# Norms of the first 768 tokens ranked among the last columns' FFN tiles, and a short convolution that starts chunk by chunk

## The chip, the cores and the metric

The kernel runs on one core of a Trainium2 chip. The metric is the device time of one execution in microseconds (us). Before the change it is 2387.01 us, the median of three runs (2381.73, 2387.01 and 2387.42).

## The reference, cut to what matters

The program is one inference step of a two-layer decoder trunk on 1032 tokens: 1024 of a prompt and 8 samples. Each layer is a mixer and a SwiGLU FFN, both closed by a LayerNorm over 1024 channels:

```
x = layernorm(ALPHA * x + mixer(x),  ln_mix_w[l], ln_mix_b[l])
x = layernorm(ALPHA * x + (silu(x @ w1) * (x @ w3)) @ w2,  ln_ffn_w[l], ln_ffn_b[l])
# mixer of layer 1, the short convolution:
p = x @ w_in                       # 1024 -> 3 * 1024: bg, cg, xv
y = bg * conv3(cg * xv);  mixer = y @ w_out
```

All of it is float32. The change touches the LayerNorm that closes the FFN in both layers, and the first tiles of the short convolution.

## The kernel before

**Data.** Activations lie transposed, channels on the 128 partitions, in three chunks of tokens: chunk 0 is tokens 0 to 383, chunk 1 is 384 to 767, chunk 2 is the other 264. `r0`, `r1` and `r2` hold the residual stream of each chunk (8 slices of 128 channels). Each float32 operand is split into a high and a low part that TensorE takes in its fast float32 form (`split`, L119: a cast on ScalarE, ACT, for the high part, a subtraction on VectorE, DVE, for the low part; both have line L120 or L121). A product is three matmuls: high weight by low activation, low by high, high by high (L141 to L143). `x0ha, x0hb, x0la, x0lb` are the parts of chunk 0's normalised input, `x1..` those of chunk 1, `x2h, x2l` those of chunk 2.

**Weights.** `load_unit` (L123) fetches one unit of 128x1024 weights (512 KB, on SyncE's queue SP) and splits it into `wh` (ACT) and `wl` (DVE). There are four buffers `raw` for the fetched units and three each for `wh` and `wl`. The first matmul of each unit reads `wl`.

**The FFN's main part.** `main_g` does chunks 0 and 1 (with fewer products, by sums of parts). Then the loop of `main` (L753) does chunk 2 in groups of four tiles of 128 hidden columns, the last group with two: `up` (L291 on DVE multiplies by silu, L283 on ACT; then the parts `hb` are split) and `down` (L266 on DVE adds to `r2`). A tile of `up` is two weight units of 24 matmuls each; a `down` of four tiles is four units, two output slices each of 12 matmuls. Layer 0 has 10 such tiles, so three groups; layer 1 has 18, so five.

**The norm.** `normalise` (L196) is a chain over engines: DVE adds the slices (L202 to L205), TensorE sums over channels (L206), DVE subtracts the mean (L216, four instructions), ACT squares (L223), DVE adds the squares (L225, L228), TensorE sums them (L231), DVE scales (L193), GpSimd (POOL) takes the power -0.5 (L194), TensorE spreads the result over the partitions (L239), DVE multiplies (L242, four instructions). Then `layer_norm` applies weight and bias (L252 on DVE, L254 on ACT) and, in layer 0, splits the eight slices for the next product (L120, L121); in layer 1 it stores them (L258).

**What sets the order.** The program is built in the order of the code, each instruction with a running number, its rank (`tc.cur_priority`). A scheduler then lays each engine's instructions in one fixed order: by its own estimate of when operands are ready, the lowest rank first. On the chip every engine works off its list in that order. Before the change the norms of chunks 0 and 1 are written after the first and the second group of the loop (L757), and so ranked there; the norm of chunk 2 comes last (L759).

**The short convolution.** `mix1` (L816) makes one tile of 128 channels: three weight units, each applied to the chunks it is given. Tiles 0 and 1 (`M1` is 2) are done for chunks 0 and 1 together (L843), then for chunk 2 alone (L845); the other tiles for all three chunks at once.

Of the kernel before, what the change touches and what calls it, by code (L numbers as in the profile page):

```python
# [31 lines left out]
NF = DFF // P  # L32
# [14 lines left out]
M1 = 2  # L47
# [21 lines left out]
def trunk(ctx: ExitStack, tc: tile.TileContext, xT, win0, wout0, win1, wout1, w1, w3, w2, vecs, sh, scf, ssc,  # L69
# [21 lines left out]
    def xp(k, c):  # L91

        if c == 2:
            return x2h[:, k, :], x2l[:, k, :]
        return X[c][k // 4][:, k % 4, :], X[c][2 + k // 4][:, k % 4, :]
# [23 lines left out]
    def split(hi, lo, src):  # L119
        SC.copy(hi, src)  # L120
        VE.tensor_tensor(lo, src, hi.bitcast(F32), ALU.subtract)  # L121

    def load_unit(src, kt, n=NK):  # L123

        wh = wsp.tile([P, NK, P], F32R, name="wh")
        wl = wsp.tile([P, NK, P], F32R, name="wl")
        raw = wsp.tile([P, NK * P], F32, name="raw", bufs=R_BUFS).rearrange("p (k f) -> p k f", f=P)
        src = src.rearrange("p (k f) -> p k f", f=P)
        for k in range(0, kt, n):
            e = min(k + n, kt)  # L130
            nc.sync.dma_start(raw[:, k:e], src[:, k:e])
            split(wh[:, k:e], wl[:, k:e], raw[:, k:e])
        return wh, wl, kt

    def mm(unit, c, parts=None):

        wh, wl, kt = unit
        ps = mmp.tile([P, 512], F32, name="mm")[:, :CH[c][1] - CH[c][0]]
        for k in range(kt):
            h, l = (parts or xp)(k, c)  # L140
            PE.matmul(ps, wl[:, k, :], h, start=k == 0, stop=False)  # L141
            PE.matmul(ps, wh[:, k, :], l, start=False, stop=False)  # L142
            PE.matmul(ps, wh[:, k, :], h, start=False, stop=k == kt - 1)  # L143
        return ps
# [44 lines left out]
    def col(i):  # L189
        return vec[:, i:i + 1]  # L190
# [113 lines left out]
    with tc.tile_pool(name="hg", bufs=1) as hg, tc.tile_pool(name="hg2", bufs=2) as hg2:  # L304
# [244 lines left out]
        for token in SCRIPT.split():  # L549
            op, gs = token[0], {"b": (1, 2)}.get(token[-1]) or (int("0" + token[1:][-1:]),)  # L550
            g, i = gs[0], int("0" + token[1:-1])
# [27 lines left out]
    ALL = (0, 1, 2)  # L579
# [12 lines left out]
    class Swiglu:  # L592
# [157 lines left out]
        def main(self, first, out):  # L750

            self.main_g(first)
            for j, m in enumerate(range(first, NF, 4)):  # L753
                ms = list(range(m, min(m + 4, NF)))
                self.up(ms, (2,))
                self.down(ms, (2,))
                if j < 2:  # L757
                    self.norm(j, out)
            self.norm(2, out)  # L759

    def t_pair(pool, j):
# [3 lines left out]
    with tc.tile_pool(name="t0", bufs=1, reuse_waits="tile") as tp:  # L765
        F0.T2, F0.T3 = t_pair(tp, 2), t_pair(tp, 3)
        with tc.tile_pool(name="head0", bufs=1, reuse_waits="tile") as act:
# [6 lines left out]
            for m in range(0, NEARLY, 4):  # L774
# [4 lines left out]
                p = tc.cur_priority  # L779
                F0.down(ms, (1, 2))  # L780
        with tc.tile_pool(name="main0", bufs=1, reuse_waits="tile") as act:
            F0.T4 = t_pair(act, 4)
            F0.main_pool(act)
            q = tc.cur_priority
# [6 lines left out]
    with tc.tile_pool(name="act", bufs=H_BUFS, reuse_waits="tile") as act:  # L791
        stt = act.tile([P, NK, 2, NS], F32, name="stt", bufs=1)
        nc.sync.dma_start(stt, ssc)
        nws = act.tile([P, NK, 2, NS], F32, name="nws", bufs=1)
        SC.copy(nws[:, :, 0, :], stt[:, :, 1, :])
        nwp = act.tile([P, NK, 2], F32, name="nwp", bufs=1)
        zhist = act.tile([P, NK, 2], F32, name="zhist", bufs=1)
        ys = {}

        def taps(i, c, z, y):  # L800

            w0, w1_, w2_ = (col(V_SC + 8 * j + i) for j in range(3))
            w = CH[c][1] - CH[c][0]
            e = w - NS if c == 2 else w
            VE.tensor_scalar(y, z[:, 2:2 + w], w2_, None, ALU.mult)
            for d, wd in ((1, w1_), (2, w0)):
                lo = d if c == 0 else 0
                VE.scalar_tensor_tensor(y[:, lo:e], z[:, 2 + lo - d:2 + e - d], wd, y[:, lo:e], ALU.mult, ALU.add)
            if c == 2:
                s = y[:, e:w]  # L810
                VE.scalar_tensor_tensor(s, stt[:, i, 1, :], w1_, s, ALU.mult, ALU.add)
                VE.scalar_tensor_tensor(s, stt[:, i, 0, :], w0, s, ALU.mult, ALU.add)
                SC.copy(nws[:, i, 1, :], z[:, 2 + e:2 + w])
                SC.copy(nwp[:, i, :], z[:, e:2 + e])

        def mix1(i, chunks):  # L816
            zs = {}
            u = load_unit(win1[8 + i], NK)
            for c in chunks:
                w = CH[c][1] - CH[c][0]  # L820
                zs[c] = act.tile([P, 386], F32, name="sl", bufs=SL_BUFS)[:, :2 + w]
                SC.copy(zs[c][:, 2:], mm(u, c))
            u = load_unit(win1[16 + i], NK)
            for c in chunks:
                z = zs[c]
                VE.tensor_tensor(z[:, 2:], mm(u, c), z[:, 2:], ALU.mult)
                if c:
                    SC.copy(z[:, 0:2], zhist[:, i, :])
                if c < 2:
                    SC.copy(zhist[:, i, :], z[:, 384:386])  # L830
                y = act.tile([P, 384], F32, name=f"y{i}{c}", tag=("hh", "hl")[(3 * i + c) % 2])
                ys[i, c] = y[:, :CH[c][1] - CH[c][0]]
                taps(i, c, z, ys[i, c])
            u = load_unit(win1[i], NK)
            for c in chunks:
                y = ys[i, c]
                VE.tensor_tensor(y, mm(u, c), y, ALU.mult)

        def parts_of(c):
            for k in range(NK):  # L840
                split(*xp(k, c), ys[k, c])

        for i in range(M1):  # L843
            mix1(i, (0, 1))
        for i in range(M1):  # L845
            mix1(i, (2,))
        for i in range(M1, NK - 1):
            mix1(i, ALL)
        for c in ALL:
            mix1(NK - 1, (c,))  # L850
            parts_of(c)
        nc.sync.dma_start(ss_o, nws)
        nc.sync.dma_start(sp_o, nwp)

    F1 = Swiglu(1)
    with tc.tile_pool(name="t1", bufs=1, reuse_waits="tile") as tp:
        F1.T2, F1.T3 = t_pair(tp, 2), t_pair(tp, 3)
        with tc.tile_pool(name="head1", bufs=1, reuse_waits="tile") as act:
# [10 lines left out]
            p = tc.cur_priority  # L869
            F1.down(ms, ALL, ALL)  # L870
        with tc.tile_pool(name="main1", bufs=1, reuse_waits="tile") as act:
            F1.T4 = t_pair(act, 4)
            F1.main_pool(act)
            q = tc.cur_priority
# [74 lines left out]
```

## Time and profile before

| what | us |
|---|---|
| median of three runs | 2387.01 |
| the profiled execution | 2385.06 |
| its span, from the first to the last instruction | 2383.2 |
| TensorE (PE) busy | 2333.2 |
| DVE busy | 1701.4 |
| ACT busy | 874.2 |

In the span, layer 0's FFN does chunk 2 from 1166.5 to 1273.6 us, and the short convolution begins there. Layer 1's FFN does chunk 2 from 2198.7 to about 2364 us. The profile gives every instruction's start, its duration, and the idle time of its engine before it with what ended that wait. Starts on one engine are a little closer than durations say, since instructions overlap at their ends.

### The profile page before, as it was taken

Reading aid. Unit: us, or ns where it says so; the run is one execution under the profiler, and the core shown is the slowest. Engines: PE = TensorE matmul, PEld = TensorE weight load, DVE = VectorE, ACT = ScalarE, POOL = GpSimd, SP = SyncE. Lnnn points to the kernel's source line nnn. Section 1 sums busy time; section 2 is a strip of 40 time slices with the busy share of each in tenths; the row PEclk is TensorE's granted clock in tenths of the full one; section 3 lists DMA queues with packets and bytes.
Section 4 is the critical chain, followed back from the end, with each engine's and each line's share of the span. In section 5 each row is a group of like instructions: output and inputs, shape, how many; then the busy total and the mean of one; then the engine's idle time right before and its main releaser. Section 6 shows DMA issues by size and latency. Waiting matters only on the chain.

```text
span 2383.2 us, 36586 instructions
## 1 busy us (share of the span) xinstructions
PE 2333.2 (98%) x14974; PEld 2293.0 (96%) x14974; DVE 1701.4 (71%) x2943; ACT 874.2 (37%) x1479; POOL 45.3 (2%) x40
## 2 busy tenths in 40 slices
PE   9999999999899999999998999999999999999997
PEld 8999899999899999999998999999999999999997
DVE  8998789897863336777686423667957777777775
ACT  5434353335631223332354211435513332332553
POOL 0000000000000000000000000000000000000000
PEclk9999999999999999999999999999999999999998
DMA  5322222453341221222342311334402222132663
GB/s 186 116 78 73 88 78 77 123 167 113 116 131 45 79 73 48 68 80 71 119 149 88 90 53 45 90 115 142 133 27 71 63 80 68 57 89 80 194 196 98
DMA packets 85560, 229.79 MB, mean 96 GB/s; under 512 B 8225, under 2 KB 26401, under 8 KB 85137
## 3 DMA queue, kind: packets, MB, share of 16 engines
q1 hardware_dynamic: 85232, 227.02, 30.9%
q8 instruction: 117, 1.92, 0.3%
q0 software_dynamic: 160, 0.45, 0.1%
q14 instruction: 51, 0.41, 0.1%
HBM read 220.22 MB, written 7.21 MB: 95 GB/s over the span
## 4 chain that ended last, share of the span: by engine, by line
PE 91%; DVE 4%; ACT 2%; POOL 1%; DMA 1%; issue 1%; SPq 0%; POOLq 0%; DVEq 0%; ACTq 0%
PE mm L141 23%; PE mm L142 23%; PE mm L143 23%; PE mm L692 6%; PE mm L693 6%; PE mm L691 6%; PE sm L335 2%; DVE wl L121 1%; POOL rs L194 1%; PE sm L239 1%; DVE r L216 1%; DVE acc L225 1%; ACT r L254 0%; PE sm L382 0%; ACT wh L120 0%
## 5 line engine op out<-in xcount | busy, mean ns | idle before, releaser
L120 ACT CAST wh<-raw 128x1024 fp32r<-128x1024 f32 (+1 forms) x466 | 468.6, 1007 | 899.4 <-PE mm L143 607.5
L121 DVE TENSOR_TENSOR wl<-raw,wh 128x1024 fp32r<-128x1024 f32 (+1 forms) x466 | 544.1, 1169 | 230.4 <-ACT wh L120 226.5
L141 PE MATMUL mm<-x2h,wl 128*128 128x264 f32 x1216 | 349.7, 288 | 7.0 <-DVE wl L121 6.9
L143 PE MATMUL mm<-x2h,wh 128*128 128x264 f32 x1216 | 346.8, 285 | 0.0
L142 PE MATMUL mm<-x2l,wh 128*128 128x264 f32 x1216 | 346.3, 285 | 0.0
L266 DVE TENSOR_TENSOR r<-r,mm 128x384 f32<-128x384 f32 (+1 forms) x336 | 171.5, 521 | 99.6 <-PE mm L143 99.2
L141 PEld LDWEIGHTS mm<-x2h,wl 128*128 128x128 f32 x1216 | 229.8, 189 | 9.6 <-DVE wl L121 8.3
L142 PEld LDWEIGHTS mm<-x2l,wh 128*128 128x128 f32 x1216 | 230.0, 189 | 1.6 <-issue 0.8
L143 PEld LDWEIGHTS mm<-x2h,wh 128*128 128x128 f32 x1216 | 229.1, 188 | 0.1
L141 PE MATMUL mm<-hb,wl 128*128 128x384 f32 (+1 forms) x672 | 211.4, 320 | 8.4 <-ACT hb L120 4.8
L142 PE MATMUL mm<-hb,wh 128*128 128x384 f32 (+1 forms) x672 | 213.1, 319 | 0.0
L143 PE MATMUL mm<-hb,wh 128*128 128x384 f32 (+1 forms) x672 | 212.8, 318 | 0.0
L482 DVE SCALAR_TENSOR_TENSOR cc<-r,vec,cc 128x256 f32<-128x256 f32 (+17 forms) x360 | 189.7, 561 | 0.9
L141 PEld LDWEIGHTS mm<-hb,wl 128*128 128x128 f32 x672 | 125.9, 190 | 10.7 <-ACT hb L120 7.0
L141 PE MATMUL mm<-x0ha,wl 128*128 128x384 f32 x384 | 132.7, 346 | 1.9 <-DVE wl L121 1.9
L143 PE MATMUL mm<-x0ha,wh 128*128 128x384 f32 x384 | 133.2, 347 | 0.0
L142 PE MATMUL mm<-x0la,wh 128*128 128x384 f32 x384 | 132.3, 345 | 0.8 <-DVE x0la L121 0.8
L143 PE MATMUL mm<-x0hb,wh 128*128 128x384 f32 x384 | 132.0, 344 | 0.0
L141 PE MATMUL mm<-x0hb,wl 128*128 128x384 f32 x384 | 131.3, 342 | 0.0
L142 PE MATMUL mm<-x0lb,wh 128*128 128x384 f32 x384 | 131.0, 341 | 0.0
L143 PE MATMUL mm<-x1hb,wh 128*128 128x384 f32 x384 | 130.8, 341 | 0.0
L142 PE MATMUL mm<-x1lb,wh 128*128 128x384 f32 x384 | 130.5, 340 | 0.0
(310 smaller groups left out, 5242.8 us busy)
## 6 DMA issues: line engine op xcount, KB each, us to landing
raw<-in_w SPq DMA_DIRECT2D x256, 512.0 KB, 3.7
raw<-in_win SPq DMA_DIRECT2D x88, 512.0 KB, 3.7
raw<-in_wout SPq DMA_DIRECT2D x48, 512.0 KB, 3.6
raw<-in_w SPq DMA_DIRECT2D x16, 256.0 KB, 2.7
out_yT<-r SPq DMA_DIRECT2D x8, 384.0 KB, 3.4
S0t<-in_sh SPq DMA_DIRECT2D x8, 256.0 KB, 3.2
out_hs<-S0t SPq DMA_DIRECT2D x8, 256.0 KB, 2.0
r<-in_xT SPq DMA_DIRECT2D x4, 384.0 KB, 7.5
```

The source lines that it names most:

```text
L120: SC.copy(hi, src)
L121: VE.tensor_tensor(lo, src, hi.bitcast(F32), ALU.subtract)
L141: PE.matmul(ps, wl[:, k, :], h, start=k == 0, stop=False)
L142: PE.matmul(ps, wh[:, k, :], l, start=False, stop=False)
L143: PE.matmul(ps, wh[:, k, :], h, start=False, stop=k == kt - 1)
L194: GP.tensor_tensor(dst, dst, mhalf[:p, :n], ALU.pow)
L266: VE.tensor_tensor(v, v, ps, ALU.add)
L335: PE.matmul(ps[:sr, c * 64:(c + 1) * 64].rearrange("p (b i) -> p b i", i=hh), kp[:, c * P:c * P + sr], qr, start=True, stop=True)
L482: VE.scalar_tensor_tensor(acc[:, lo:W], u[:, 30 + lo - d:30 + W - d], col(V_DW + (30 - d) * 4 + i), acc[:, lo:W], ALU.mult, ALU.add)
L691: PE.matmul(ps, w[1][:, k], t[0][:, k], start=k == 0, stop=False)
L692: PE.matmul(ps, w[0][:, k], t[1][:, k], start=False, stop=False)
L693: PE.matmul(ps, w[0][:, k], t[0][:, k], start=False, stop=k == 3)
```

## The change

The loop over chunk 2's groups has no norm in it any more. After the loop the norms of chunks 0 and 1 are written with a rank of their own: one third and two thirds of the way from the loop's first rank to its last. In the short convolution, tiles 0 and 1 are done for chunk 0, then for chunk 1, then for chunk 2, each time with the weight units loaded anew: 18 units in place of 12.

```diff
             self.main_g(first)
-            for j, m in enumerate(range(first, NF, 4)):
+            p = tc.cur_priority
+            for m in range(first, NF, 4):
                 ms = list(range(m, min(m + 4, NF)))
                 self.up(ms, (2,))
                 self.down(ms, (2,))
-                if j < 2:
-                    self.norm(j, out)
+            q = tc.cur_priority
+            for c in (0, 1):
+                tc.cur_priority = p + (q - p) * (c + 1) // 3
+                self.norm(c, out)
+            tc.cur_priority = q
             self.norm(2, out)
...
-        for i in range(M1):
-            mix1(i, (0, 1))
-        for i in range(M1):
-            mix1(i, (2,))
+        for c in ALL:
+            for i in range(M1):
+                mix1(i, (c,))
```

The order on DVE shows what this does. In it `r0_73`, `r1_5697` and `r2_74` are the residuals of chunks 0, 1 and 2, `mm_` is a result of TensorE, `wl_` the low part of a weight unit, `hb_` a part of a hidden tile, `acc_` and `sq_` sums and squares of a norm.

**Place 1, layer 0, the `down` of the first group.** DVE before:

```order
L266 TENSOR_TENSOR r2_74<-r2_74,mm_11564 128x264
L266 TENSOR_TENSOR r2_74<-r2_74,mm_11578 128x264
L121 TENSOR_TENSOR wl_11725<-raw_11726,wh_11724 128x1024
L266 TENSOR_TENSOR r2_74<-r2_74,mm_11598 128x264
L266 TENSOR_TENSOR r2_74<-r2_74,mm_11612 128x264
L121 TENSOR_TENSOR wl_11758<-raw_11759,wh_11757 128x1024
L266 TENSOR_TENSOR r2_74<-r2_74,mm_11632 128x264
L266 TENSOR_TENSOR r2_74<-r2_74,mm_11646 128x264
L216 TENSOR_TENSOR r0_73<-r0_73,sm_11661 128x768 x4
```

And now:

```order
L266 TENSOR_TENSOR r2_74<-r2_74,mm_11564 128x264
L266 TENSOR_TENSOR r2_74<-r2_74,mm_11578 128x264
L216 TENSOR_TENSOR r0_73<-r0_73,sm_12287 128x768 x4
L225 TENSOR_TENSOR acc_12295<-acc_12295,sq_12299 128x768
L266 TENSOR_TENSOR r2_74<-r2_74,mm_11598 128x264
L266 TENSOR_TENSOR r2_74<-r2_74,mm_11612 128x264
L266 TENSOR_TENSOR r2_74<-r2_74,mm_11632 128x264
L225 TENSOR_TENSOR acc_12295<-acc_12295,sq_12303 128x768
L266 TENSOR_TENSOR r2_74<-r2_74,mm_11646 128x264
L121 TENSOR_TENSOR wl_11661<-raw_11662,wh_11660 128x1024
```

The norm of chunk 0 starts two weight units earlier, in the middle of the group; the split of the next `up`'s first unit, which stood ahead of the norm (`wl_11725`), now stands behind its L216, two L225 and four L266 (`wl_11661`).

**Place 2, layer 0, the end of chunk 1's norm.** DVE before, beside the last `up`:

```order
L193 TENSOR_SCALAR rs_12144<-sm_12143 96x4
L121 TENSOR_TENSOR wl_12378<-raw_12376,wh_12377 128x1024
L242 TENSOR_TENSOR r1_5697<-r1_5697,sm_12167 128x768 x4
L252 TENSOR_SCALAR r1_5697<-r1_5697,vec_133 128x384
L121 TENSOR_TENSOR x1la_81<-r1_5697,x1ha_79 128x384 x2
L291 TENSOR_TENSOR hb_12275<-mm_12308,hb_12275 128x264
L121 TENSOR_TENSOR x1la_81<-r1_5697,x1ha_79 128x384 x2
L121 TENSOR_TENSOR x1lb_82<-r1_5697,x1hb_80 128x384
L121 TENSOR_TENSOR wl_12488<-raw_12489,wh_12487 128x1024
L121 TENSOR_TENSOR x1lb_82<-r1_5697,x1hb_80 128x384 x2
L121 TENSOR_TENSOR hb_12335<-hb_12275,hb_12334 128x264
```

And now, beside the `down` of the second group:

```order
L193 TENSOR_SCALAR rs_12358<-sm_12357 96x4
L121 TENSOR_TENSOR wl_12073<-raw_12074,wh_12072 128x1024
L242 TENSOR_TENSOR r1_5697<-r1_5697,sm_12381 128x768 x4
L252 TENSOR_SCALAR r1_5697<-r1_5697,vec_133 128x384
L121 TENSOR_TENSOR x1la_81<-r1_5697,x1ha_79 128x384 x4
L121 TENSOR_TENSOR x1lb_82<-r1_5697,x1hb_80 128x384
L266 TENSOR_TENSOR r2_74<-r2_74,mm_12024 128x264
L266 TENSOR_TENSOR r2_74<-r2_74,mm_12044 128x264
L266 TENSOR_TENSOR r2_74<-r2_74,mm_12058 128x264
L121 TENSOR_TENSOR x1lb_82<-r1_5697,x1hb_80 128x384 x2
L121 TENSOR_TENSOR wl_12106<-raw_12107,wh_12105 128x1024
```

The norm of chunk 1 now ends before the last `up` (`wl_12073` is that `up`'s first unit, `wl_12106` its second); the last hidden tile's L291 and `hb` no longer stand among its instructions.

**Place 3, layer 1, the end of chunk 0's norm.** DVE before, beside an `up`:

```order
L193 TENSOR_SCALAR rs_21246<-sm_21245 96x4
L121 TENSOR_TENSOR wl_21462<-raw_21463,wh_21461 128x1024
L242 TENSOR_TENSOR r0_73<-r0_73,sm_21269 128x768 x4
L252 TENSOR_SCALAR r0_73<-r0_73,vec_133 128x384
L291 TENSOR_TENSOR hb_21365<-mm_21398,hb_21365 128x264
L121 TENSOR_TENSOR wl_21498<-raw_21499,wh_21497 128x1024
```

And now, beside the `down` of the second group:

```order
L193 TENSOR_SCALAR rs_22732<-sm_22731 96x4
L266 TENSOR_TENSOR r2_74<-r2_74,mm_21556 128x264
L266 TENSOR_TENSOR r2_74<-r2_74,mm_21570 128x264
L266 TENSOR_TENSOR r2_74<-r2_74,mm_21590 128x264
L242 TENSOR_TENSOR r0_73<-r0_73,sm_22755 128x768 x4
L252 TENSOR_SCALAR r0_73<-r0_73,vec_133 128x384
L266 TENSOR_TENSOR r2_74<-r2_74,mm_21604 128x264
L266 TENSOR_TENSOR r2_74<-r2_74,mm_21624 128x264
L266 TENSOR_TENSOR r2_74<-r2_74,mm_21638 128x264
L121 TENSOR_TENSOR wl_21654<-raw_21652,wh_21653 128x1024
```

The norm has moved from an `up` into a `down`, and the split of that `down`'s last unit (`wl_21654`) stands behind the norm's L242.

## Rows read from the trace of the kernel before

**Rows 1.** The page: busy time, share of the span and instructions of each engine.
```profile
PE 2333.2 (98%) x14974; PEld 2293.0 (96%) x14974; DVE 1701.4 (71%) x2943; ACT 874.2 (37%) x1479; POOL 45.3 (2%) x40
```

**Rows 2.** Waits, 1189 to 1274 us: who, for whom, total us, times, longest.
```profile
PE mm L141 <- DVE hb L291: 3.3, 1, 3.3
PE mm L141 <- ACT hb L120: 2.7, 1, 2.7
...
PE mm L141 <- DVE wl L121: 2.2, 2, 1.6
```

**Rows 3.** Waits of PE, 2183 to 2365 us, chunk 2 of layer 1.
```profile
PE sm L239 <- POOL rs L194: 2.1, 2, 1.0
```

**Rows 4.** Timeline of PE: start, us, instruction, count, [idle before <-releaser].
```profile
1224.40 0.39 PE L141 MATMUL mm<-x2h,wl 128*128 128x264 f32 x1 [1.64 <-DVE wl L121]
...
1228.15 0.39 PE L141 MATMUL mm<-x2h,wl 128*128 128x264 f32 x1 [0.58 <-DVE wl L121]
...
1263.30 0.59 PE L141 MATMUL mm<-hb,wl 128*128 128x264 f32 x1 [3.34 <-DVE hb L291]
...
1267.03 1.25 PE L141 MATMUL mm<-hb,wl 128*128 128x264 f32 x4 [2.70 <-ACT hb L120]
```

**Rows 5.** Timeline of DVE, the same places, columns as in rows 4.
```profile
1262.82 0.42 DVE L291 TENSOR_TENSOR hb<-mm,hb 128x264 f32<-128x264 f32 x1
...
1267.01 0.43 DVE L121 TENSOR_TENSOR hb<-hb 128x264 fp32r<-128x264 f32 x1 [0.19 <-ACT hb L120]
```

**Rows 6.** Windows: stretch, us, busy (count) of PE PEld DVE ACT POOL, PEclk, DMA, GB/s.
```profile
1189.69:1201.54 11.85, 11.82 (x99) 11.60 (x98) 8.23 (x13) 4.52 (x5) 0.00 (x0) 1.00 0.60 178
1262.60:1272.50 9.90, 6.50 (x28) 6.19 (x29) 7.77 (x17) 5.84 (x12) 0.00 (x0) 0.50 0.21 61
620.70:624.10 3.40, 3.40 (x18) 3.40 (x18) 3.00 (x4) 0.14 (x1) 0.00 (x0) 0.51 0.71 195
1216.20:1219.60 3.40, 3.40 (x31) 3.40 (x30) 3.12 (x4) 2.61 (x5) 0.00 (x0) 1.00 0.49 158
...
1202.00:1268.00 66.00, 55.64 (x439) 53.54 (x438) 59.18 (x86) 42.42 (x67) 3.91 (x2) 0.96 0.46 139
1300.00:1325.00 25.00, 25.00 (x146) 25.00 (x145) 9.04 (x13) 4.57 (x9) 0.00 (x0) 1.00 0.26 85
```

**Rows 7.** Timeline of DVE, 1195 to 1222 us: `down`, then the norm of chunk 0.
```profile
1195.72 0.76 DVE L266 TENSOR_TENSOR r<-r,mm 128x264 f32<-128x264 f32 x2
...
1202.38 3.54 DVE L216 TENSOR_TENSOR r<-r,sm 128x768 f32<-128x768 f32 x4 [0.22 <-PE sm L206]
1205.85 0.95 DVE L225 TENSOR_TENSOR acc<-acc,sq 128x768 f32<-128x768 f32 x1
...
1213.17 1.23 DVE L121 TENSOR_TENSOR wl<-raw,wh 128x1024 fp32r<-128x1024 f32 x1
1216.48 3.55 DVE L242 TENSOR_TENSOR r<-r,sm 128x768 f32<-128x768 f32 x4 [2.09 <-PE sm L239]
...
1220.33 1.02 DVE L121 TENSOR_TENSOR x0la<-r,x0ha 128x384 fp32r<-128x384 f32 x2
```

**Rows 8.** Timeline of POOL, the power -0.5 of chunk 0's norm.
```profile
1213.30 1.96 POOL L194 TENSOR_TENSOR rs<-rs,mhalf 96x4 f32<-96x4 f32 x1 [573.09 <-DVE rs L193]
```

**Rows 9.** Timeline of PE, the matmul L239 that waits for it, chunks 0, 1, 2.
```profile
1215.31 1.13 PE L239 MATMUL sm<-ident,rs 96*128 96x96 f32 x8 [1.04 <-POOL rs L194]
...
1256.86 0.91 PE L239 MATMUL sm<-ident,rs 96*128 96x96 f32 x6 [1.04 <-POOL rs L194]
...
1288.58 0.90 PE L239 MATMUL sm<-ident,rs 88*128 88x88 f32 x6 [0.22 <-POOL rs L194]
```

**Rows 10.** Timeline of ACT beside that norm: the cast of a weight unit.
```profile
1201.73 1.05 ACT L120 CAST wh<-raw 128x1024 fp32r<-128x1024 f32 x1 [1.82 <-PE mm L143]
```

**Rows 11.** Timeline of PE, two other waits.
```profile
548.80 0.88 PE L239 MATMUL sm<-ident,rs 96*128 96x96 f32 x3 [2.12 <-POOL rs L194]
...
619.77 0.39 PE L141 MATMUL mm<-x2h,wl 128*128 128x264 f32 x1 [3.62 <-DVE wl L121]
```

## The prediction, made before the changed kernel ran

> **What bounds the kernel now.** I read the engines' busy shares first: PE is busy 2333 of 2383 us, so what can be won lies in some 50 us of PE's idle time and in stretches at a lower clock [rows 1]. Next the waits of PE, window by window. In layer 0's last chunk (1189 to 1274 us) it waits four times over for DVE's or ACT's splits (8.2 us) and twice for POOL [rows 2, 9]; in layer 1's last chunk only twice for POOL, 2.1 us in all [rows 3]. Then PE's timeline gives the places: 1.64 and 0.58 us for a weight split, 1.04 twice at L239, and 3.34 and 2.70 us at the `down` after the last `up` [rows 4, 9]. The sum is 10.34 us. DVE's timeline gives the reason: while PE stands from about 1260 to 1263.3, DVE reaches the L291 that PE needs only at 1262.82, and the low part `hb` only at 1267.01, because chunk 1's norm is ahead of them on its list [rows 5]. From 1202 to 1268 DVE is busy 59 of 66 us [rows 6]: with two norms laid over this stretch DVE, not PE, is nearly its bound. After the 3.34 us wait the granted clock is 0.50, which is the lower of the two levels (1.2 GHz), until 1272.5; 28 matmuls take 6.50 us of PE there [rows 6], and at the 0.123 us of the `down` before (11.85 us for its 96 matmuls [rows 6]) they would take 3.4. So 3.1 us go to the clock, and the close of layer 0 loses 13.4 us in all. That is what the change can win there.
>
> **The price list.** A step is the time to the next start, about 0.09 less than the duration: four L216 3.47, four L242 3.46, L225 0.87, L266 or L291 or an `hb` split 0.34, an x split 0.47, a weight split 1.13 (ready after 1.22) [rows 7]. L202 and L204 have L225's form and go at its price, L252 at 0.4 (half an L225). From L231 to L239 lies POOL's 1.96 [rows 8]; L242 starts 1.17 after L239 [rows 7, 9]. A matmul over chunk 2 is 0.123.
>
> **Part 1, layer 0's close.** The order shows that the norms do move. I follow DVE's new list against PE's, wait by wait.
>
> (a) First `down` (place 1). L206 now runs in the middle of the 96 matmuls, at about 1195.9, so L216 can start at 1196.7 (0.84 later, as 1202.38 follows 1201.54). Ahead of `wl_11661` stand 3.47 + 2 x 0.87 + 4 x 0.34 = 6.6 us: 1203.3, ready at 1204.5. PE ends the `down` at 1201.54 plus some 0.6 for the L206 inside it, 1202.1. PE waits 2.4. Before, this split was two units ahead.
>
> (b) L239 of chunk 0 again has 10 matmuls of cover behind L231, so 1.04 again; a weight split now stands right before L193: 1.3.
>
> (c) Between L242 and the split of the second next unit stand 3.46 + 0.4 + eight x splits 3.8 + two L291 0.7 + an `hb` 0.3 + one weight split 1.1 + two L204 1.7 = 11.5 us. With L242's lag 1.17, half a us of waiting for ACT's casts and 1.22 for the split itself it is ready 14.4 us after L239. PE's work in that time is L239 (0.9) and 89 matmuls, 11.7. It waits 2.7; before, 1.64 + 0.58 here.
>
> (d) Second `down`: from L206 to its third unit PE has 0.6 + 45 x 0.123 = 6.1 us; DVE has 0.84 + 3.47 + 0.34 + four L266 1.36 + two L225 1.74 + 1.22 = 9.0. PE waits 2.7 to 2.9; I take 2.7.
>
> (e) L239 of chunk 1 has 4 matmuls of cover, not 10: 1.04 + 6 x 0.123 = 1.8.
>
> (f) Place 2: from L239 DVE needs 1.17 + 3.46 + 0.4 + seven x splits 3.3 + three L266 1.0 + 1.22 = 10.6 us until `wl_12106` is there; PE has 0.9 + 47 x 0.123 = 6.7. It waits 4.0 (3.9).
>
> (g) What the change aims at: the `down` after the last `up` has nothing of a norm ahead of its L291. One weight split (`wl_12488`) is left before the last `hb`: 0.3 in place of 3.34 + 2.70.
>
> Sum: 2.4 + 1.3 + 2.7 + 2.7 + 1.8 + 4.0 + 0.3 = 15.2 us against 10.34. The norms' DVE work is the same, 17 us each; it is only moved from beside an `up` into a `down`, where each unit carries two more L266.
>
> Then the clock. In the trace the waits of 2.12, 3.34 and 3.62 us were each followed at once by a stretch at the lower level [rows 4, 6, 11] (after the 2.12 three L239 take 0.88 us, after a wait of 1.04 eight take 1.13 [rows 9, 11]); those of 1.64 and 1.04 in layer 0's close by none. Some shorter waits elsewhere were followed by one too, so the border isn't sharp. At the lower level 18 matmuls run in 3.40 us (from 620.7), at the higher 31 (from 1216.2) [rows 6], so one such stretch costs 13 x 0.12 = 1.5 us. Five new waits lie above 2.1 us: (a), (c), (d), (f), and the last of part 3. I take three stretches, 4.5 us, since a slower PE gives DVE time to catch up; none and five are the bounds, 0 and 7.5.
>
> Layer 0 without the clock: 15.2 - 13.4 = +1.8. Bounds: -9 (only (g) is right and the new waits shrink to the old ones) and +4 (half a us more at each).
>
> **Part 2, the short convolution.** PE does the same matmuls in another order. Six weight units more mean six DMAs of 512 KB on SP, six casts of 1.05 on ACT [rows 10] and six splits of 1.13 on DVE. Here DVE is busy 9 of 25 us and DMA moves 85 GB/s [rows 6]; a unit per 24 matmuls of 384 columns (25 us per 146, so 4.1 us) is 128 GB/s, against 178 in the first `down` [rows 6]. I price them at nothing. Where chunk 2's norm lies over them DVE is fuller: then at most the six splits show, 6.8. L239 of chunk 2 has 4 matmuls of cover in place of 6: 0.22 grows by 2 x 0.17 to 0.56 [rows 9], +0.35. That chunk 1's input isn't needed for 25 us wins nothing, since PE never waited for it there.
>
> **Part 3, layer 1's close.** Only chunk 0's norm changes its surroundings; chunk 1's keeps the shape that it had (L206 at the start of an `up`, 10 matmuls between L231 and L239), one group later: 1.04 as before. Chunk 0's norm: `wl` of the first unit of the second `down` stands behind four L216 and one L225, 0.5 us late; L239 with a weight split ahead of L193 1.3; and place 3: from L239 DVE needs 1.17 + 3.46 + 0.4 + three L266 1.0 + 1.22 = 7.3 until `wl_21654`, PE has 0.9 + 28 x 0.123 = 4.3, so 2.9 us. That is 4.7 against 1.04: +3.7, bounds 0 and +5. The four stores of chunk 0 move on SP ahead of five weight loads; four `raw` buffers cover them, nothing.
>
> **The sum.** +1.8 + 0.35 + 3.7 + 4.5 = +10.3 us on the profiled execution's 2385.06 (its span 2383.2 and 1.9 around it): 2395.4. That execution is 2.0 below the median of the three runs, 2387.01, so it would be 8.4 above that median, 0.35%.
>
> **A rule of the Trainium skill.** While POOL works (1213.30 to 1215.26) a weight split with two SBUF inputs runs beside it on DVE, from 1213.17, and takes 1.23 us, no more than its price elsewhere [rows 7, 8]. The Trainium skill's page "SBUF — State Buffer" (section "Who interferes with whom") says that a DVE instruction with two SBUF inputs contends with a GpSimd instruction that reads SBUF, and that the loser is blocked. By that rule the L202 and weight splits that now stand beside the two L194 would be up to 1.96 us late each time, and the sum would be some 4 us more. The row shows none of it, and I add nothing.
>
> **The rivals.** *The new waits close up* (0.30): the waits of part 1 shift one another, PE slowed at one place finds the next split ready, and no or one stretch at the lower clock comes. For it: DVE's work per chunk is unchanged and it is the bound, so it ends about when it did. Against it: the chains of (d), (e), (f) start from PE itself, so a late PE makes DVE late too. Then part 1 gives 0, part 3 half, +2, in all about +2.5: 2387.5.
>
> *The gain of (g) comes through* (0.10): it is decided at place 1 and place 2. If the weight split after the norm's first half is done when PE ends the `down` (if DVE's 6.6 us there were 4.3), the wait (a) is gone, and with no long wait no stretch at the lower clock. Then (g) and its clock win 3.34 + 2.70 + 3.1 - 0.3 = 8.8 us, part 3 and L239 take back 1: 2377.3. For it: in the trace the norm and an `up` side by side cost only 3.3 us of waits. Against it: the same prices from rows 7 give the waits above.
>
> *The moved norms change nothing* (0.05): what DVE can't do in one place it does in another, 2385 to 2387.
>
> **How the numbers follow.** My own case has 0.55: 2395.4, by its own bounds 2390 to 2402. About 0.3% is what a measurement of this kernel can tell from no change; against the median that is 2379.9 to 2394.2. Slower: most of my case, 0.50, and 0.03 of the first rival (its splits of part 2 showing), 0.53. Same: the rest of my case 0.05, 0.27 of the first rival and the last rival's 0.05, 0.37. Faster: 0.10. For the range I take 2383 to 2404: it leaves out the faster rival and what lies beyond five stretches with part 2's splits showing.
>
> **What would show it.** Right: a wait of PE for `wl` of 2 us or more where layer 0's second group begins, one in the second `down`, one of about 4 us before the second unit of the last `up`, no wait over 1 us at the `down` after it; in layer 1 a wait of about 3 us in the second `down`; the first short convolution matmul 1 to 7 us later than 1273.6. Wrong: that matmul before 1270, or PE's waits for `wl` in layer 1 absent. If instead waits appear in the first 60 us of the short convolution, part 2 was mis-sized.

## The result

The changed kernel takes 2397.53 us (median of 6 runs, 2392.39 to 2399.71), the kernel before beside it 2385.11 (median of 6, 2381.73 to 2387.42). The ratio is 1.0053, with a 95% interval of 1.0041 to 1.0066: slower by about 12 us. The forecast was 2395.4, slower. The profiled execution took 2399.31 us (span 2397.4), which is at the upper end of its runs; a second profile (below) caught one at 2393.7.

The engines of the changed kernel, from the page; it answers to [rows 1]:

```profile
PE 2343.4 (98%) x14974; PEld 2304.8 (96%) x14974; DVE 1707.9 (71%) x2949; ACT 879.7 (37%) x1485; POOL 43.6 (2%) x40
```

PE does the same 14974 matmuls and is busy 10.2 us longer, so some of them ran slower. Where the rest went is found by cutting both spans at three matmuls that both have: the first of chunk 2's groups in layer 0, the first of the short convolution, and the first of chunk 2's groups in layer 1.

| stretch | before, us | after, us | difference |
|---|---|---|---|
| start to chunk 2's groups, layer 0 | 1166.50 | 1164.87 | -1.63 |
| close of layer 0 | 107.10 | 116.56 | +9.46 |
| short convolution and layer 1 up to chunk 2's groups | 925.06 | 925.72 | +0.66 |
| close of layer 1, to the end | 184.59 | 190.30 | +5.71 |

The windows view of the two closes, the kernel before (columns as in [rows 6]):

```profile
1166.50:1273.60 107.10, 96.71 (x758) 94.26 (x758) 84.96 (x124) 58.70 (x88) 3.91 (x2) 0.95 0.48 144
2198.66:2383.25 184.59, 169.72 (x1367) 166.51 (x1366) 126.99 (x184) 85.18 (x119) 4.76 (x3) 0.96 0.51 160
```

And of the changed kernel, with four of its slow stretches ahead:

```profile
1203.06:1211.50 8.44, 8.44 (x46) 8.44 (x47) 5.80 (x7) 1.32 (x2) 1.65 (x1) 0.60 0.64 186
1225.26:1228.75 3.49, 3.49 (x17) 3.49 (x18) 3.03 (x4) 0.63 (x2) 0.00 (x0) 0.55 0.57 159
...
1263.62:1269.30 5.68, 5.68 (x26) 5.68 (x27) 2.77 (x3) 1.35 (x2) 0.00 (x0) 0.50 0.73 200
...
2280.30:2285.90 5.60, 5.60 (x25) 5.60 (x26) 3.51 (x4) 0.55 (x1) 0.00 (x0) 0.50 1.02 351
...
1164.87:1281.43 116.56, 104.29 (x757) 101.72 (x757) 84.42 (x124) 58.65 (x88) 3.57 (x2) 0.90 0.45 132
2207.15:2397.45 190.30, 172.93 (x1367) 169.48 (x1366) 127.29 (x184) 85.07 (x119) 3.81 (x3) 0.94 0.51 156
```

DVE does the same work (84.96 and 84.42 us in layer 0's close), in 9.46 us more. PE's busy time there grew by 7.58, at a granted clock of 0.90 in place of 0.95; in the last two of the stretches above it is 0.50, the lower level (1.2 GHz). So most of the loss in this execution is clock, and the rest of it is waiting. PE's waits stand where the prediction put them. The waits view of PE, 1188 to 1281 us, which answers to [rows 2]:

```profile
PE mm L141 <- DVE wl L121: 10.4, 4, 3.1
PE sm L239 <- POOL rs L194: 1.7, 1, 1.7
```

And one by one on PE's timeline, which answers to [rows 4, 9]:

```profile
1203.06 0.39 PE L141 MATMUL mm<-x2h,wl 128*128 128x264 f32 x1 [2.35 <-DVE wl L121]
...
1225.26 0.59 PE L141 MATMUL mm<-x2h,wl 128*128 128x264 f32 x1 [2.39 <-DVE wl L121]
...
1244.87 0.39 PE L141 MATMUL mm<-hb,wl 128*128 128x264 f32 x1 [2.59 <-DVE wl L121]
...
1252.12 1.90 PE L239 MATMUL sm<-ident,rs 96*128 96x96 f32 x8 [1.73 <-POOL rs L194]
...
1263.62 0.59 PE L141 MATMUL mm<-x2h,wl 128*128 128x264 f32 x1 [3.06 <-DVE wl L121]
...
1297.26 0.90 PE L239 MATMUL sm<-ident,rs 88*128 88x88 f32 x6 [0.73 <-POOL rs L194]
...
2266.62 0.39 PE L141 MATMUL mm<-hb,wl 128*128 128x264 f32 x1 [0.43 <-DVE wl L121]
...
2280.30 0.59 PE L141 MATMUL mm<-hb,wl 128*128 128x264 f32 x1 [2.76 <-DVE wl L121]
```

The 3.34 and 2.70 us of [rows 4] at the last `down` are gone, and five waits of 12.12 us together stand in layer 0's close in place of six of 10.34. Each of the four for `wl` is read on DVE's list; the first, which answers to [rows 7], and the last:

```profile
1195.23 3.54 DVE L216 TENSOR_TENSOR r<-r,sm 128x768 f32<-128x768 f32 x4 [0.37 <-PE sm L206]
1198.70 0.95 DVE L225 TENSOR_TENSOR acc<-acc,sq 128x768 f32<-128x768 f32 x1
1199.57 1.10 DVE L266 TENSOR_TENSOR r<-r,mm 128x264 f32<-128x264 f32 x3
1200.58 0.95 DVE L225 TENSOR_TENSOR acc<-acc,sq 128x768 f32<-128x768 f32 x1
1201.45 0.42 DVE L266 TENSOR_TENSOR r<-r,mm 128x264 f32<-128x264 f32 x1
1201.79 1.22 DVE L121 TENSOR_TENSOR wl<-raw,wh 128x1024 fp32r<-128x1024 f32 x1
...
1254.07 3.55 DVE L242 TENSOR_TENSOR r<-r,sm 128x768 f32<-128x768 f32 x4 [2.86 <-PE sm L239]
...
1257.92 2.02 DVE L121 TENSOR_TENSOR x1la<-r,x1ha 128x384 fp32r<-128x384 f32 x4
...
1260.33 1.10 DVE L266 TENSOR_TENSOR r<-r,mm 128x264 f32<-128x264 f32 x3
...
1262.35 1.22 DVE L121 TENSOR_TENSOR wl<-raw,wh 128x1024 fp32r<-128x1024 f32 x1
```

PE's matmuls at 1203.06 and 1263.62 start as these splits end, and DVE has no gap ahead of any of the four splits. Its idle 2.86 us at 1254.07 is the other half: the norm itself waited for PE and POOL.

### The profile page after: what moved, and what is told of

Its sections match the earlier page's. It is cut to its first block, busy times and chain, and to the rows that moved or that the text cites. A ratio compares the mean times of both kernels' runs of the same rounds, so it can differ in the third digit from the quotient of the medians.

```text
span 2397.4 us, 36616 instructions
## 1 busy us (share of the span) xinstructions
PE 2343.4 (98%) x14974; PEld 2304.8 (96%) x14974; DVE 1707.9 (71%) x2949; ACT 879.7 (37%) x1485; POOL 43.6 (2%) x40
## 3 DMA queue, kind: packets, MB, share of 16 engines
q8 instruction: 117, 1.92, 0.3%
## 4 chain that ended last, share of the span: by engine, by line
PE 91%; DVE 5%; ACT 2%; POOL 1%; DMA 1%; issue 1%; SPq 0%; POOLq 0%; DVEq 0%; ACTq 0%
PE mm L141 23%; PE mm L142 23%; PE mm L143 23%; PE mm L692 6%; PE mm L693 6%; PE mm L691 6%; PE sm L335 2%; DVE wl L121 1%; POOL rs L194 1%; DVE r L216 1%; PE sm L239 1%; DVE acc L225 1%; ACT r L254 0%; PE sm L382 0%; DVE r L242 0%
## 5 line engine op out<-in xcount | busy, mean ns | idle before, releaser
L120 ACT CAST wh<-raw 128x1024 fp32r<-128x1024 f32 (+1 forms) x472 | 474.8, 1007 | 891.3 <-PE mm L143 575.4
L121 DVE TENSOR_TENSOR wl<-raw,wh 128x1024 fp32r<-128x1024 f32 (+1 forms) x472 | 551.8, 1171 | 237.2 <-ACT wh L120 233.7
L141 PE MATMUL mm<-x2h,wl 128*128 128x264 f32 x1216 | 353.6, 291 | 12.8 <-DVE wl L121 12.7
L141 PEld LDWEIGHTS mm<-x2h,wl 128*128 128x128 f32 x1216 | 234.5, 193 | 15.4 <-DVE wl L121 14.7
L266 DVE TENSOR_TENSOR r<-r,mm 128x384 f32<-128x384 f32 (+1 forms) x336 | 170.4, 521 | 98.0 <-PE mm L143 97.4
L141 PE MATMUL mm<-hb,wl 128*128 128x384 f32 (+1 forms) x672 | 213.0, 322 | 8.1 <-DVE wl L121 5.8
L141 PEld LDWEIGHTS mm<-hb,wl 128*128 128x128 f32 x672 | 127.1, 191 | 10.8 <-DVE wl L121 6.4
L141 PE MATMUL mm<-x0ha,wl 128*128 128x384 f32 x384 | 131.3, 342 | 1.7 <-DVE wl L121 1.7
L141 PE MATMUL mm<-x1hb,wl 128*128 128x384 f32 x384 | 131.4, 342 | 0.0
L141 PE MATMUL mm<-x0hb,wl 128*128 128x384 f32 x384 | 130.8, 341 | 0.0
```

The source lines that it names most:

```text
L266: VE.tensor_tensor(v, v, ps, ALU.add)
```

## The experiments

The theory (A): DVE takes its list in order, the change puts pieces of a norm ahead of the weight splits that the next units need, PE waits, and part of the matmuls behind a wait run at the lower clock. The rivals: the six more weight units (B); DVE is full, whatever its order (C); the parts act on each other (D).

**The three parts of the change, each alone on the kernel before.** First only the short convolution:

```diff
-        for i in range(M1):
-            mix1(i, (0, 1))
-        for i in range(M1):
-            mix1(i, (2,))
+        for c in ALL:
+            for i in range(M1):
+                mix1(i, (c,))
```

> The kernel before, with only the short convolution's first two tiles chunk by chunk. Theory A (the loss is DVE's order at the two closes of an FFN: weight splits behind pieces of a norm, PE waits for them and the clock falls after the waits): the six more weight units are hidden, +0 to +0.7 us on before; layer 0's close keeps its 3.34 and 2.70 us waits; no wait of PE for a weight split in the first 60 us of the short convolution. Rival B (the six more weight units and the chunk-wise order cost it): +5 to +9 us, with waits for weights there. Rival C (DVE is simply full, its order doesn't matter): +0 to +0.7, as A.

Measured: 2383.71 us, before 2384.06, ratio 1.0003 (0.9994 to 1.0012). PE's long waits in layer 0's close are those of before:

```profile
PE mm L141 <- DVE hb L291: 3.3, 1, 3.3
...
PE mm L141 <- ACT hb L120: 2.7, 1, 2.7
```

In the short convolution PE waits once, 0.75 us for L239 of chunk 2. The six units are hidden; rival B, which expected +5 to +9 us here, falls as the cause.

Then only the ranks, in layer 0 (and the same with `self.l == 1`):

```diff
             self.main_g(first)
+            if self.l == 0:
+                ...
+                for c in (0, 1):
+                    tc.cur_priority = p + (q - p) * (c + 1) // 3
+                    self.norm(c, out)
+                tc.cur_priority = q
+                self.norm(2, out)
+                return
```

> The kernel before, with only layer 0's norms ranked among the columns' tiles; layer 1 and the short convolution as before. Theory A: +6 to +9 us; the waits of 2.35, 2.39, 2.59 and 3.06 us in layer 0's close are there as in the changed kernel, each followed by a stretch with a granted clock of 0.5 to 0.6. Rival B: +0 to +2. Rival D (the two closes act on each other, or the clock of the whole run moves): the sum of this run, of the one for layer 1 and of the one for the short convolution differs from the changed kernel's +12.4 by more than 3 us; by A the three add up to it.

Measured: 2388.85 us, ratio 1.0022 (1.0011 to 1.0032), +5.2 us, a little under what A expected. The four waits for `wl` are there (2.35, 2.38, 2.55, 2.72), but not each is followed by a lower clock: behind the first two it is 1.00, behind the other two 0.63 and 0.69. The windows behind the second and over the whole close:

```profile
1221.31:1225.00 3.69, 3.69 (x30) 3.69 (x31) 3.43 (x5) 1.06 (x3) 0.00 (x0) 1.00 0.62 158
...
1163.07:1274.59 111.52, 98.92 (x757) 96.13 (x757) 84.33 (x124) 58.64 (x88) 3.57 (x2) 0.95 0.47 138
```

After 2.38 us of waiting the clock is 1.00 here; after 2.39 at the same place it was 0.55 in the changed kernel's profile (1225.26 to 1228.75). PE is busy 98.92 us in this close, 5.4 less than there, with the waits all but equal. Part of that is the choice of the execution: this profile is of one of the faster ones (2385.35 us), that of the changed kernel of a slower one.

> The kernel before, with only layer 1's norms ranked among the columns' tiles. Theory A: +4 to +6 us; one wait of about 2.8 us for a weight split near 2280 us and a stretch at the lower clock behind it. Rival B: 0.

Measured: 2387.33 us, ratio 1.0013 (1.0003 to 1.0023), +3.1 us, under the 4 to 6 expected. The wait, on PE's timeline, is the changed kernel's to a hundredth, and in the 4.75 us behind it the clock is 0.64:

```profile
2271.55 0.59 PE L141 MATMUL mm<-hb,wl 128*128 128x264 f32 x1 [2.76 <-DVE wl L121]
```

**Both ranks, and the whole change again.** The parts give 0.7 + 5.2 + 3.1 = 9.0 us by their ratios, the whole 12.6. That is 3.6 us apart, over the 3 us that the expectation had set as the sign of rival D, though each of the four ratios is itself uncertain by 2 to 3 us. Two runs look at the difference: the changed kernel with the short convolution as before (the first diff above, reversed), and the changed kernel once more.

> The changed kernel's norms in both layers, but the short convolution's first tiles as before. Theory A (the parts add up): +5.2 and +3.2 us of the two single runs, so +6 to +11 us on before, and within 2 us of the changed kernel. Rival D (the edit of the short convolution costs something only beside the later norm of chunk 2): 3 us or more under the changed kernel.

> The changed kernel once more, with a second profile. Theory A (the waits are set by the order and come again to a tenth of a us; how much of the clock is lost behind them varies from run to run): the same six waits in layer 0's close and the same 2.8 us in layer 1's, but another sum of lower-clock stretches; +8 to +12 us on before on this chip, within 2 us of the run with both closes ranked. Rival D (the short convolution's edit costs 3 us or more beside the ranked norms): 3 us or more above that run, with waits after layer 0's close that it doesn't have.

Measured: both ranks 2393.40, before 2383.20, ratio 1.0048 (1.0033 to 1.0063). The change again 2396.92, before 2384.57, ratio 1.0057 (1.0043 to 1.0071). By their ratios that is 11.4 and 13.6 us, a little over what A expected (6 to 11 and 8 to 12). The waits of the second profile are 2.35, 0.73, 2.38, 2.55, 1.74 and 3.07, all but the 0.73 as in the first, to 0.04 us. The clock is not. Behind the first, behind the last, and over the two closes:

```profile
1202.04:1204.90 2.86, 2.86 (x25) 2.86 (x25) 2.86 (x4) 0.00 (x0) 0.00 (x0) 1.00 0.59 170
...
1260.50:1266.20 5.70, 5.70 (x26) 5.70 (x27) 2.79 (x4) 1.36 (x3) 0.00 (x0) 0.50 0.73 205
...
1163.85:1278.31 114.46, 101.48 (x757) 98.69 (x757) 84.41 (x124) 58.65 (x88) 3.57 (x2) 0.93 0.44 134
2203.99:2391.84 187.85, 170.62 (x1367) 167.09 (x1366) 127.37 (x184) 85.10 (x119) 3.81 (x3) 0.96 0.51 158
```

So the same kernel with the same waits lost 5.1 us less to the clock in this execution (101.48 + 170.62 against 104.29 + 172.93). The mean granted clock on record goes with the times of the first six runs as well: 0.985 in the three of 2399.3 to 2399.7 us, 0.987 at 2395.76, 0.989 at 2393.43 and 2392.39. So the clock is most of what spreads them over 7 us.

Whether the short convolution's edit adds 2 us beside the ranked norms (1.0057 against 1.0048) isn't settled by the times: the intervals overlap. The traces leave little room for it. Cut at the same matmuls, the stretch from the short convolution to layer 1's chunk 2 takes 924.44 us in the run with both ranks and 925.68 in the second profile of the change, and PE's only wait in its first 60 us is that for L239, 0.36 and 0.73 us. The 3 us or more that rival D expected there aren't seen. That the two ranks together cost more than each alone (11.4 against 5.2 + 3.1) is neither shown nor excluded; rival D stays open at that size.

**The splits ahead of the norm's pieces.** The changed kernel, where only the weight units of chunk 2's loop are ranked earlier, so that DVE's list gets its splits ahead of the pieces of L216, L225 and L242 (the same two lines stand around the load in the FFN's `down`):

```diff
+    ahead = [0]
     def load_unit(src, kt, n=NK):
...
+        tc.cur_priority -= ahead[0]
         for k in range(0, kt, n):
             ...
+        tc.cur_priority += ahead[0]
...
+            ahead[0] = 150
             for m in range(first, NF, 4):
                 ...
+            ahead[0] = 0
```

> The changed kernel, where in the loop over the last columns' tiles each weight unit's load, cast and split are ranked 150 steps earlier, so that on DVE they stand ahead of the pieces of the norm that were ahead of them; the norms stay where the change put them. Theory A: the waits for weight splits of over 2 us shrink below 1 us and most of the stretches at the lower clock go with them; 6 to 14 us under the changed kernel, so -3 to +6 us on before. Rival C (DVE is full in these 66 us, another order only moves the waits): waits of the same sum stand at L239 or at `hb`, and the time stays at +9 to +13 us on before. Rival E (earlier loads find no free buffer, and the loads queue on SP): new waits for DMA before `wh` casts, slower than the changed kernel.

Measured: 2384.70 us, ratio 1.0005 (0.9996 to 1.0014): 11 to 12 us under the changed kernel, level with before. Waits of PE in layer 0's close, and its windows row:

```profile
PE mm L145 <- DVE r L270: 3.6, 2, 2.8
PE mm L145 <- DVE wl L121: 2.9, 2, 2.0
PE mm L145 <- ACT hb L120: 1.4, 1, 1.4
```

```profile
1167.08:1271.91 104.83, 95.60 (x758) 93.02 (x757) 84.77 (x124) 58.80 (x88) 2.01 (x2) 0.98 0.47 147
```

(Line numbers shift in this kernel; L145 is L141, L270 is L266.) The waits for splits fell from 10.4 to 2.9 us, with one of 2.00 left where A expected none over 1. Part came back as waits for residuals (3.6), as C would have it: with the smaller ones, PE's waits in this close are 9.1 us, against 12.1 in the changed kernel. But PE is busy only 95.60 us, 8.7 less than in the changed kernel's first profile and 5.9 less than in its second. DVE's 84.77 us are the same work. So the order decides, and C falls: it expected +9 to +13. The edit moves the loads and ACT's casts forward too; but those hadn't held up the splits, since DVE had no gap ahead of them.

**The norms one group earlier.** The kernel before with the norm of chunk 0 ahead of the first group, and that of chunk 1 ahead of the second, in both layers:

```diff
             for j, m in enumerate(range(first, NF, 4)):
                 ms = list(range(m, min(m + 4, NF)))
+                if j < 2:
+                    self.norm(j, out)
                 self.up(ms, (2,))
                 self.down(ms, (2,))
-                if j < 2:
-                    self.norm(j, out)
```

> The kernel before, with each of the two norms one group earlier: norm of chunk 0 ahead of the first group's `up`, norm of chunk 1 ahead of the second group's `up`, in both layers; nothing else. Theory A (what costs is DVE work of a norm beside a short stretch of PE work that needs a new split for every unit): the waits of 3.34 and 2.70 us at the last `down` of layer 0 and the stretch at the lower clock behind them go, since both norms now lie beside an `up` of four tiles; each leaves about 1.04 + 1.64 + 0.58 as chunk 0's norm does before, 6.5 in place of 10.3; 4 to 9 us under before. Rival C (DVE is full over the whole close, its order doesn't matter): the same sum of waits elsewhere, 0 +- 2. Rival F (the norm of chunk 0 now meets the last residuals of the loop over chunks 0 and 1): a new wait of 2 us or more at the first `up` of chunk 2, time at before +2 to +6.

Measured: 2379.39 us, before 2383.20, ratio 0.9981 (0.9971 to 0.9992), 4.5 us faster. All waits of PE in layer 0's close of more than 0.4 us, and its windows row:

```profile
1186.13 0.39 PE L141 MATMUL mm<-x2h,wl 128*128 128x264 f32 x1 [2.21 <-DVE wl L121]
...
1189.95 0.39 PE L141 MATMUL mm<-hb,wl 128*128 128x264 f32 x1 [0.65 <-DVE wl L121]
...
1215.36 1.13 PE L239 MATMUL sm<-ident,rs 96*128 96x96 f32 x8 [1.04 <-POOL rs L194]
...
1224.45 0.39 PE L141 MATMUL mm<-x2h,wl 128*128 128x264 f32 x1 [1.63 <-DVE wl L121]
...
1228.45 0.39 PE L141 MATMUL mm<-x2h,wl 128*128 128x264 f32 x1 [0.82 <-DVE wl L121]
```

```profile
1160.66:1261.31 100.65, 94.13 (x757) 91.51 (x757) 84.07 (x124) 58.26 (x88) 3.08 (x2) 1.00 0.50 153
```

6.35 us of waits, as A had it (6.5), and a clock of 1.00 over the whole close. This is where the change wanted to go: nothing of a norm is left beside the last `up`. The 2.21 us wait is the new one that rival F spoke of (of 2 us or more at chunk 2's first `up`), but it is the only one of that length and no stretch of lower clock follows here. This profile is of the fastest of the 11 executions (2372.76 us, 6.6 under their median), and 5.8 us of its lead over the profile of before lie ahead of the close; so it shows the waits, but not what the clock does in the median run.

**Both together**, the norms one group earlier and the weight units ranked 150 steps earlier (shown against the kernel of the last run; the lines around the loads are as above):

```diff
                 if j < 2:
                     self.norm(j, out)
+                ahead[0] = 150
                 self.up(ms, (2,))
                 self.down(ms, (2,))
+                ahead[0] = 0
```

> The norms one group earlier, and the weight units of chunk 2's loop ranked 150 steps earlier as in the run with splits ahead. Theory A: the 1.64 and 0.58 us waits for splits shrink as well; 2 to 4 us under the version with the norms one group earlier alone, 6 to 12 under before. Rival: with the splits first, the residuals and L291 of the running group come later, as in the run with splits ahead (3.6 us of waits there for L266's residuals), and nothing is won over the norms one group earlier alone.

Measured: 2375.54 us, ratio 0.9969 (0.9957 to 0.9980): 7.4 us faster than before, and some 20 faster than the changed kernel. Its layer 0 close:

```profile
1164.03:1264.25 100.22, 94.54 (x757) 91.70 (x757) 83.87 (x124) 58.31 (x88) 2.13 (x2) 1.00 0.50 154
```

PE's longest wait in it is 1.25 us. That it beats the norms moved alone isn't shown: the two intervals overlap, and the closes differ by 0.43 us.

## Why the prediction was right, and which of its terms were not

The mechanism, its places and the sign were right. That the sum came out right too is luck, since two terms missed in opposite directions: the waits grew by 4.7 us where the forecast had 8.9, the clock cost about 7.7 more where it had 1.4. One of the signs that it named missed as well: the first matmul of the short convolution, forecast 1 to 7 us after 1273.6, came 7.8 after it in the first profile and 4.7 in the second.

- **The waits of layer 0.** Predicted against measured: (a) 2.4, 2.35; (b) 1.3, none in the first profile and 0.73 in the second; (c) 2.7, 2.39; (d) 2.7, 2.59; (e) 1.8, 1.73; (f) 4.0, 3.06; (g) 0.3, none. The sum 15.2 came to 12.1, so the waits alone grew by 1.8, where the forecast had 15.2 - 10.34 = 4.9 before the clock. In (b) and (f) a term was left out that the prediction named only in general: a PE that runs at the lower clock gives DVE time. Between 1203.06 and the L239 of (b) PE was at 0.60 and came after POOL had ended. In the second profile PE was at 1.00 there, and POOL's power, beside an L202 of 0.94 us, took 1.65 us in place of 1.96, which is about half of what the 0.73 falls short of 1.3. In (f) PE, slowed behind (e), took 8.4 us from L239 to the wait where 6.7 was forecast. In (c) the working has a slip: 0.9 + 89 x 0.123 is 11.85, not 11.7, so its prices give 2.55, nearer to the 2.39.
- **The waits of layer 1.** Predicted +3.7: 0.5, 1.3 and 2.9 against 0.43, 0.09 and 2.76. Measured +2.3. The 1.3 failed for another reason, below.
- **The short convolution.** Predicted +0.35, measured +0.66 for the whole stretch; L239 of chunk 2 waits 0.73 where 0.56 was forecast and 0.22 was before [rows 9].
- **The clock.** This term was mis-sized. The forecast was three stretches of 1.5 us, 4.5, less the 3.1 that go at the old place: +1.4. In the first profile PE's busy time in the two closes grew by 7.58 + 3.21 = 10.8 us, in the second by 4.77 + 0.90 = 5.7. The medians leave 12.4 less the waits (1.8 + 2.3 + 0.66), about 7.7; that is an estimate, since the waits are those of the first profile. Stretches are longer than the one that was taken as the measure, 3.40 us from 620.7 [rows 6]: 26 matmuls in 5.68 and 25 in 5.60, where at 0.123 they take 3.2 and 3.1, so 2.5 each. And the wait of (e), 1.73 us, had one too (L239 took 1.90 in place of 1.13), though it lies under the 2.1 us above which the prediction counted waits.
- **The first rival** (the waits close up, 2387.5) was nearer on the waits (its whole sum was +2.5; they came to +4.7, and the forecast without the clock had +8.9): it failed on the clock. **The second** (the gain of (g) comes through) was decided where it said, at place 1: DVE's 6.6 us ahead of that split took 6.56 (1195.23 to 1201.79).
- **The rule that was set aside.** The prediction held that the row of a weight split of 1.23 us beside POOL [rows 7, 8] shows no contention. It looked at the wrong engine. POOL's rows in the changed kernel:

```profile
1208.36 1.65 POOL L194 TENSOR_TENSOR rs<-rs,mhalf 96x4 f32<-96x4 f32 x1 [568.66 <-DVE rs L193]
1250.15 1.92 POOL L194 TENSOR_TENSOR rs<-rs,mhalf 96x4 f32<-96x4 f32 x1 [40.14 <-DVE rs L193]
...
2271.93 1.00 POOL L194 TENSOR_TENSOR rs<-rs,mhalf 96x4 f32<-96x4 f32 x1 [577.91 <-DVE rs L193]
```

The power at 1250.15 starts beside a weight split (1249.99, 1.21 us) and takes 1.92; the one at 2271.93 starts beside an L266, which has one of its inputs in PSUM, and takes 1.00. So the 1.96 of [rows 8], used as POOL's price, already held about 1 us of contention, and where DVE happened to do something else it was gone: the 1.3 of layer 1 became 0.09. Adding 4 us for the rule would have counted it twice.

## What to carry to other kernels

On an engine that takes its list in order, moving a block of work earlier puts it ahead of whatever small step the next unit needs: list, for each such step, what now stands in front of it, and put the steps that another engine waits for first. In this kernel a block of side work cost least beside the longest stretch of the main engine's work that has its operands ready (the four-tile `up`), and more beside the one where each unit brings two more duties (`down`). Price a wait of PE at more than its length, since in some executions the matmuls behind it run at half the clock (0.50 here), and read a contended operation's price on both of the engines.

## What the runs showed of the hardware that was not expected

To measure POOL's price alone, a tail was added to the kernel before: four powers (96x4) on POOL at a time, first next to a DVE that has little to do, then next to 12 subtractions of two SBUF tiles (one of which DVE ran beside the first four powers, so that 11 are left), then 24 additions with one input in PSUM, then 24 scalings with one SBUF input.

```diff
...
+        powers(1)
+        for i in range(12):
+            VE.tensor_tensor((bc, bd)[i % 2], ba, bb, ALU.subtract)
+        gate()
+        powers(2)
+        for i in range(24):
+            VE.tensor_tensor((bc, bd)[i % 2][:, :256], ba[:, :256], bp_[:, :256], ALU.add)
+        gate()
+        powers(3)
+        for i in range(24):
+            VE.tensor_scalar((bc, bd)[i % 2][:, :512], ba[:, :512], 2.0, None, ALU.mult)
```

> The kernel before with a tail: four times four POOL powers (96x4), first beside an idle DVE, then beside subtractions of two SBUF tiles (128x1024, the form of a weight split), then beside additions with one input in PSUM (128x256), then beside scalings with one SBUF input. Theory G (POOL loses to a DVE instruction with two SBUF inputs): about 1.0 us each beside an idle DVE, PSUM additions and scalings, 1.6 to 2.0 beside the subtractions. Rival H (the length of L194 depends on something else, such as what POOL did before it): the same length in all four, or the first of each four longer than the rest. The time itself says nothing, since the tail is added work of some 50 us.

Measured (2427.57 us with the tail). POOL's timeline, each row four powers:

```profile
2383.15 4.79 POOL L895 TENSOR_TENSOR brs<-brs,mhalf 96x4 f32<-96x4 f32 x4 [6.93 <-DVE brs L898]
2388.28 16.20 POOL L895 TENSOR_TENSOR brs<-brs,mhalf 96x4 f32<-96x4 f32 x4 [0.33 <-DVE brs L898]
2404.81 3.93 POOL L895 TENSOR_TENSOR brs<-brs,mhalf 96x4 f32<-96x4 f32 x4 [0.33 <-DVE brs L898]
2412.90 11.76 POOL L895 TENSOR_TENSOR brs<-brs,mhalf 96x4 f32<-96x4 f32 x4 [4.16 <-DVE brs L898]
```

DVE beside it, the last subtraction, an addition, and the last scaling:

```profile
2399.48 1.21 DVE L905 TENSOR_TENSOR bd<-ba,bb 128x1024 f32<-128x1024 f32 x1
...
2404.66 0.41 DVE L909 TENSOR_TENSOR bc<-ba,mm 128x256 f32<-128x256 f32 x1
...
2420.46 0.42 DVE L913 TENSOR_SCALAR bd<-ba 128x512 f32<-128x512 f32 x1
```

Beside additions from PSUM a power takes 3.93 / 4 = 0.98 us. Beside the subtractions the four took 16.20: DVE's last one ends at 2400.69, and the 3.79 us from there to POOL's end are four undisturbed powers (the view of a shorter window has the first of the four at 13.27 us by itself). So POOL stood still for the whole 12.4 us of 11 subtractions in a row, not for one of them, while each subtraction kept its 1.21 us. Theory G had the right loser and far too small a price (1.6 to 2.0 us each), and it was wrong on the scalings: with one SBUF input they block POOL as well (11.76 us, of which 3.78 lie after the last scaling's end at 2420.88). Rival H, the same length in all four groups or a longer first power in each, falls with these rows. The first row's 0.86 us above the third's comes with the one subtraction that runs beside it.

The Trainium skill's page "SBUF — State Buffer" (section "Who interferes with whom") names both kinds of DVE instruction, those with two SBUF inputs and `tensor_scalar` in a two-port mode, and says that the one that comes second is fully blocked. These rows agree on who comes second and is blocked, though the trace doesn't name the mode of the scalings; they add that a row of such instructions on DVE lets POOL in at no point between them.

That the same wait at the same place (2.39 and 2.38 us) is followed by a clock of 0.55 in one execution and 1.00 in another was the other surprise. In the four profiles that have these waits (the changed kernel twice, layer 0's ranks alone, both ranks) the clock behind the first is 0.60 once and 1.00 three times, behind the second 0.55, 0.60 and twice 1.00, behind the last three of the close between 0.50 and 0.70 each time. What decides between them isn't settled by these runs.
